# A one-core transformer block: weight steps paced by product, each unit's first product moved up one place, and a reload cut into pieces

## The chip, the core and the metric

The kernel runs on one core of a Trainium2 chip. A core has engines that run side by side, each with its own queue of instructions in a fixed order: TensorE (PE) multiplies matrices, VectorE (DVE) and ScalarE (ACT) work on whole tiles, GpSimd (POOL) is little used here, and SyncE (SP) issues all transfers between the core's memory and DRAM. An engine that comes to an instruction whose inputs are not there stands still, with all that is queued behind it. PE writes its sums into PSUM banks of 128 x 512 numbers, and ACT and DVE take them out.

The metric is the device time of one execution in microseconds (us). The kernel before takes 2230.76 us, the median of three runs (2227.21 to 2230.81).

## What is computed

The input is a matrix x of 1024 tokens x 1024 features, in 32-bit floats. The block normalises it, projects it with one wide matrix, mixes tokens in two ways, merges, and adds a squared-ReLU network:

```python
xn = rmsnorm(x, norm1_g[l])
qa, ka, va, qr, kr, vr, gr, gate_a, gate_b = [xn @ wl[:, bounds[i]:bounds[i + 1]] for i in ...]
# o_a: dilated sliding-window attention, 12 heads of 128, mixed over three groups
# o_r: retention, 4 heads, keys of 256, values of 512, in chunks of 128 tokens
y = jax.nn.sigmoid(gate_a) * (o_a @ w_proj_a[l]) + jax.nn.sigmoid(gate_b) * (o_r @ w_proj_b[l])
x = x + y @ w_out[l]
x = x + jnp.square(jax.nn.relu(rmsnorm(x, norm2_g[l]) @ w_up[l])) @ w_down[l]
```

## The kernel before, in words

**Numbers in two parts.** Every operand of a large product is split into a high part (`wh`, `xh`), which ACT writes as a rounded copy (line 330), and a low part (`wl`, `xl`), which DVE writes as the difference (line 333). A product of two such operands takes three matmuls: high x high, high x low and low x high.

**Units of seven products.** The projections from the normalised input, the second projection and the up projection are done in units of 256 output features with a fast scheme in the manner of Strassen: seven products N1 to N7 instead of eight. A product is 12 matmuls (4 blocks of the sum x 3). N1 and N2 of a unit are summed in one PSUM bank, N6, N7 and N4 in a second, N5 and N3 in a third (`BANK`). The bank of N6, N7 and N4 begins as minus N1: ACT copies N1's result there, negated (line 398), and only then may N2 go on summing on N1's bank. N6 and N7 are copied out by ACT too (lines 403 and 406).

**Order on PE.** PE's order is the program's. `strassen_order` gives it: two units' N1 and N2 first, then for each unit j the products N6, N5, the N1 of unit j+2, N7, the N2 of unit j+2, N4 and N3. There are 36 input units, 252 products: the q and k of the 12 attention heads (a unit for each head), eight units of the retention's gate `gr`, eight of the merging gates, and eight of the retention's q and k (`rqk`). The second projection (eight units, called "pb") has its own list in the same order. The other engines' orders are made by a scheduler from the program's order, except for instructions that are told to keep their place.

**Weights.** The class `Weights` holds a list of weight steps. A unit has two raw tiles of 512 KB each, loaded by SP (line 182) into a ring, and four steps: A is for N1 and N2, and D, B and C for the rest. C is for N5 and N7. A step splits one raw tile, or half of one, into its two parts; behind step D, DVE also forms the sums of the raw quarters (line 123) that B and C need. There are two buffers for A, two for B, and one for C. When a product was the last user of a buffer, `free` calls `pump`, which carries out all steps whose buffer is free, requesting raw tiles as the ring allows. So a split can be put in order directly behind the request of its own raw tile.

**Attention beside the units.** From product 138 on, the 12 heads' attention runs in small matmuls between those of the unit products. `plan_core` hangs actions on product numbers (`on(p, ...)`). For head n with p0 = 138 + 9 n, the q and k of its first 512 tokens (c = 0) are requested at p0 - 4 and those of the last (c = 1) at p0. `scale` multiplies q (f = 0) or k (f = 1) on DVE by its norm (line 705); it was due at p0 - 2 and p0 - 1 for c = 0, and at p0 + 2 and p0 + 3 for c = 1. Scores (line 642) need the scaled q and k. DVE adds a bias and takes the minimum (line 645), ACT takes the exponential (line 647), PE turns the result, ACT copies it out (line 657, `pT`), and PE multiplies by the values.

**Where the retention begins.** The retention needs the fourth quarter of the normalised input, `XS[0, 1]`, in its chunks 4 to 7 of each head. It was put aside in DRAM (`xs_d`) when its place was wanted, and is loaded back as two transfers of 1 MB (line 910). Each of the 32 chunks needs its q and k (`rqT`, `rkT`, 128 KB each, line 902) from DRAM; PE uses them at line 933. They are issued two chunks ahead.

Stages: start and values up to about 141 us, input units 141 to 971 (attention from 557), retention to 1310, first projection to 1340, second projection to 1490, output projection to 1605, up to 1890, down to the end.

Of the kernel before, what the change touches and what calls it, by code (L numbers as in the profile page):

```python
# [10 lines left out]
F = mybir.dt.float32  # L11
# [26 lines left out]
class Weights:  # L38
# [12 lines left out]
    def __init__(self, nc, rawp, wp, split):  # L51
        self.nc, self.rawp, self.wp, self.split = nc, rawp, wp, split
        self.raw, self.used, self.next = [], set(), 0
        self.src, self.steps = [], []
        self.place, self.more = [], None
        self.last = {}
        self.units, self.done = {}, set()
        self.plain = self.taken = 0
        self.cycle, self.turn = tuple(range(self.WB)), 0

        self.places = {}
        self.limit, self.keep, self.first = None, None, {}

    def claim(self, buf, key):

# [30 lines left out]
    def add_units(self, tag, srcs, flip=0):  # L96

        base = len(self.src)
        self.first[tag] = len(self.steps)
        kept = {}  # L100
        for s in srcs:
            self.place += [(len(self.src) + i - base) % (self.RAW + 1) for i in range(2)]
            self.src += [s[0], s[1]]

        def piece(key, buf, r, cols, then=None):
            def step():
                if isinstance(buf, tuple):
                    if not kept:
                        kept["D"] = self.buffer(buf[0])
                    h, l = (x[:, 512 * buf[1]:512 * buf[1] + 512] for x in kept["D"])  # L110
                else:
                    h, l = self.buffer(buf)
                self.split(h, l, self.raw[r][:, cols], key[0] == "up" and key[1] < 2 and key[2] != "A")
                self.units[key] = h, l
                if then:
                    then()

            self.steps.append((self.claim(buf, key), r, step))

        def sums(r):  # L120
            (x22, x21), (x11, x12) = ((self.raw[i][:, 0:512], self.raw[i][:, 512:1024]) for i in (r, r + 1))
            for x, y in ((x22, x21), (x21, x11), (x11, x22), (x12, x11)):
                ins = self.nc.vector.tensor_tensor(x, x, y, op=OP.add)
                if tag == "up" and r <= base + 2:
                    self.keep(ins)

        both = slice(0, 1024)
        for j in range(-1, len(srcs)):
            if j + 1 < len(srcs):
                r = base + 2 * (j + 1)  # L130
                piece((tag, j + 1, "A"), self.A[(j + 1) % 2], r + 1, both)
            if j >= 0:
                r = base + 2 * j
                piece((tag, j, "D"), (self.D, j % 2), r, slice(0, 512), lambda r=r: sums(r))
                piece((tag, j, "B"), self.B[(j + flip) % 2], r + 1, both, lambda r=r: self.used.add(r + 1))
                piece((tag, j, "C"), self.C, r, both, lambda r=r: self.used.add(r))
        m = len(srcs) + flip
        self.cycle = (0, 1, self.B[m % 2], self.C, self.D, self.B[(m - 1) % 2])
        self.turn = 0
# [32 lines left out]
    def load(self):  # L172
        n = len(self.raw)
        if n >= len(self.src):
            return False
        b = self.place[n]
        if any(self.place[m] == b and m not in self.used for m in range(max(0, n - 8), n)):
            return False
        if b == self.RAW and self.more is None:
            return False  # L180
        raw = (self.more if b == self.RAW else self.rawp).tile([P, UW], F, name=f"raw{b}", bufs=1)
        self.nc.sync.dma_start(raw[:, :self.src[n].shape[1]], self.src[n])
        self.raw.append(raw)
        return True

    def pump(self, most=99):
        while most > 0 and self.next < len(self.steps) and self.next != self.limit:
            before, r, step = self.steps[self.next]
            if before - self.done:
                return  # L190
            while len(self.raw) <= r:
                if not self.load():
                    return
            step()
            self.next += 1
            while self.load():
                pass
            most -= 1
# [4 lines left out]
        return list(range(lo, lo + count))  # L203

    def __getitem__(self, i):
        return self.units[i]

    def free(self, *ids):
        self.done.update(ids)
        self.pump()  # L210


class Pipe:


    def __init__(self, nc):
        self.nc = nc
        self.slot = 0
        self.due = {}

# [17 lines left out]
    def step(self, ps, terms, ends=None, first=True):  # L238
        fns = self.due.pop(self.slot, [])
        n, m = len(terms), len(fns)  # L240
        place = {}
        for j, fn in enumerate(fns):
            place.setdefault(min(n - 1, (j + 1) * n // (m + 1)), []).append(fn)

        def after(i):
            for fn in place.get(i, []):
                fn()
            if ends and i in ends:
                ends[i]()

        self.group(ps, terms, after, first)
        self.slot += 1

# [5 lines left out]
BANK = {"N1": "a", "N2": "a", "N6": "b", "N7": "b", "N4": "b", "N5": "d", "N3": "d"}  # L261


def strassen_order(units):


    order = [(0, "N1"), (1, "N1"), (0, "N2"), (1, "N2")]
    for j in range(units):
        late = j + 3 >= units
        order += [(j, "N6"), (j, "N5")] + ([] if late else [(j + 2, "N1")]) + [(j, "N7")]  # L270
        order += [(j + 2, "N2")] if not late else [(units - 1, ("N1", "N2")[j + 3 - units])] if j + 1 < units else []
        order += [(j, "N4"), (j, "N3")]
    return order
# [3 lines left out]
def hybrid_block(ctx: ExitStack, tc: tile.TileContext, a: dict, out: bass.AP):  # L277
    nc = tc.nc
# [89 lines left out]
    for nb in range(2):  # L368
        for u in range(4):
# [5 lines left out]
                 [{"N1": 0, "N2": 1, "N3": 2, "N5": "n2a", "N7": "n2b", "N6": 5, "N4": 4},  # L375
                  {"N1": "y1a", "N2": "n3a", "N3": "n3b", "N5": 3, "N7": "w1a", "N6": "w1b", "N4": "w1c"}])
    pipe = Pipe(nc)

    def product(tag, j, name, unit, operands, pu, result):

# [294 lines left out]
    def plan_core():  # L675
# [62 lines left out]
        for n in range(HEADS):  # L738
            p0 = FIRST + EACH * n
            on(p0 - 1, lambda n=n: prepare(n))  # L740
            for c in range(2):
                on(p0 - 4 + 4 * c, lambda n=n, c=c: bring(n, c))
                for f in range(2):
                    on(p0 - 2 + 4 * c + f, lambda n=n, c=c, f=f: scale(n, c, f))
            for b in range(NT):
                p, m = p0 + b, NT * n + b
                if b % 2 == 0:
                    on(p, lambda n=n, b=b: fetch(n, b))
                on(p, lambda n=n, b=b: begin(n, b))
                on(p, lambda m=m: pipe.at(3, lambda: turned(m)))  # L750
                on(p, lambda m=m: pipe.at(0, stages[m][0]))
# [16 lines left out]
    with ExitStack() as ph:  # L768
# [74 lines left out]

        unit = {}
        NIN = NA + NG + NQ + 8
        first = W.take(4)
        for p, (j, name) in enumerate(strassen_order(NIN)):
            if p == FIRST - 4:
                sqs.close()
                plan_core()  # L850
            for fn in events.pop(p, []):
                fn()
            product("in", j, name, unit, operands, lambda: pu, result)
            if (j, name) == (NIN - 1, "N7"):
                start = values(first, slice(0, P), False)
        assert not events
        W.more = None
    gst.close()


# [25 lines left out]
    with ExitStack() as ph:  # L886
# [19 lines left out]

        load_chunk(0)
        load_chunk(1)
        for i, x in enumerate(XS[0, 1]):
            tc.keep_in_program_order(nc.sync.dma_start(x.bitcast(F).rearrange("p a b -> p (a b)"), xs_d[i]))  # L910
        places = [x for i in range(2) for x in as_rows(XS[i, 0])]
        oaS = [(places[2 * p][:, i], places[2 * p + 1][:, i]) for p in range(2) for i in range(2)]

# [5 lines left out]
        for h in range(RH):  # L919
# [4 lines left out]
            for c in range(NT):  # L924
                ts = slice(c * P, (c + 1) * P)
                load_chunk(NT * h + c + 2)
                qT, kT, sr = ready.pop(NT * h + c)
                it = {}

# [112 lines left out]
    with ExitStack() as ph:  # L1042
        ES, e1, exts = None, ExitStack(), ExitStack()
        OPB = [{"N5": XS[0, 1], "N7": XS[1, 1]}, {}]
        waiting = [("N7", 1)] + [(name, h) for name in ("N1", "N2", "N6") for h in range(2)]
        sigmoid(gates[0])
        for n, (d, cs) in enumerate(work):
            if not cs.start:
# [39 lines left out]
        pm3 = pool(ph, "pm3", 10)  # L1088
        order = [(0, "N1"), (1, "N1"), (0, "N2"), (1, "N2")]
        for j in range(6):  # L1090
            order += [(j, "N6"), (j, "N5"), (j + 2, "N1"), (j, "N7"), (j + 2, "N2"), (j, "N4"), (j, "N3")]
        order += [(6, "N6"), (6, "N5"), (6, "N7"), (7, "N6"), (6, "N4"), (7, "N5"), (7, "N7"), (6, "N3"), (7, "N4"),
                  (7, "N3")]
        results = [(j, *{"N2": (0, 0), "N7": (1, 1), "N4": (1, 0), "N3": (0, 1)}[name])
# [60 lines left out]
        for i, (j, name) in enumerate(order):  # L1155
# [11 lines left out]
            if (j, name) in fetched:  # L1167
                u = fetched[j, name]
                late[u] = loaded(pm3, yl_d[u - 4], "s")
        assert not todo and not begun and not late  # L1170
        e1.close()


# [387 lines left out]
```

## Time and profile before

| | before |
|---|---|
| median of three runs | 2230.76 us |
| the profiled execution | 2229.98 us |
| its span, first to last instruction | 2228.2 us |
| granted TensorE clock, mean | 0.996 |
| busy: PE, DVE, ACT, POOL | 2174.8, 1390.9, 1127.4, 330.5 us |
| moved by DMA | 359.09 MB, 161 GB/s on average |

How to read the rows of the next sections. A row of a timeline gives start, length, engine, line of the kernel, operation, output and inputs with sizes, and in brackets the idle time before it and what ended it. SPq rows are transfers issued by SP. A row of waits gives the engine, its tile and line, what it waited for, the total in us, how often, and the longest. A row of stages gives the window, its length, for PE, PE's weight loads, DVE, ACT and POOL the busy time with the number of instructions, then the granted clock, the DMA share and GB/s. "mm" and "ms" are the PSUM banks of products, "tr" those of small matmuls and transposes.

### The profile page before, as it was taken

To read this page: it belongs to the slowest core of one execution; us is meant where nothing else is said; L and a number is where in the kernel's file an instruction comes from. 1 tells how busy PE (TensorE), PEld (TensorE's weight loads), DVE (VectorE), ACT (ScalarE), POOL (GpSimd) and SP (SyncE) were. 2 spreads that over 40 slices of the span, in tenths; PEclk is the share of its full clock that TensorE was granted. 3 is DMA by queue.
4 is the path that set the end of the run, shared out by engine and by line. 5 is a ranking of instruction groups with operands and counts; after the bars stand their busy time and mean duration, and the time that the engine had idled before them with its cause. 6 is when DMAs were issued, how large, how long until landed. Compare 5 with 4: busy or idle time off the path is not lost. (4 is left out here: it accounts for less than half of the span.)

```text
span 2228.2 us, 28853 instructions
## 1 busy us (share of the span) xinstructions
PE 2174.8 (98%) x9928; PEld 1785.4 (80%) x9928; DVE 1390.9 (62%) x2374; ACT 1127.4 (51%) x2145; POOL 330.5 (15%) x340
## 2 busy tenths in 40 slices
PE   8999999999999999999999999999899999999999
PEld 6888888787888888878888877778788888778777
DVE  5624554655555665648776867793855556787874
ACT  4425665544654544535555645552555545755542
POOL 0000000000000000002133120000000000677873
PEclk9999999999999999999999999999999999999999
DMA  6323333333657667664364478774255556644533
GB/s 205 133 85 91 99 102 97 96 133 111 199 169 219 207 197 216 186 193 129 113 199 119 133 254 267 258 239 153 86 147 154 153 149 201 225 166 160 179 122 104
DMA packets 293750, 359.09 MB, mean 161 GB/s; under 512 B 34962, under 2 KB 202322, under 8 KB 293091
## 3 DMA queue, kind: packets, MB, share of 16 engines
q1 hardware_dynamic: 293602, 357.25, 51.2%
q8 instruction: 78, 1.28, 0.2%
q14 instruction: 70, 0.57, 0.1%
HBM read 240.59 MB, written 116.59 MB: 160 GB/s over the span
## 5 line engine op out<-in xcount | busy, mean ns | idle before, releaser
L333 DVE TENSOR_TENSOR wl<-raw,wh 128x1024 fp32r<-128x1024 f32 (+1 forms) x308 | 345.4, 1123 | 384.9 <-ACT wh L330 384.2
L330 ACT ACTIVATE wh<-raw 128x1024 fp32r<-128x1024 f32 (+1 forms) x308 | 295.8, 962 | 278.7 <-PE ms L229 98.1
L229 PE MATMUL mm<-xh,wh 128*128 128x512 f32 x960 | 390.4, 407 | 10.2 <-ACT ms L398 9.7
L229 PE MATMUL mm<-xh,wl 128*128 128x512 f32 x960 | 376.3, 392 | 0.0
L229 PE MATMUL mm<-xl,wh 128*128 128x512 f32 x960 | 376.0, 392 | 0.3 <-DVE xl L333 0.3
L229 PE MATMUL ms<-xh,wh 128*128 128x512 f32 x784 | 317.5, 405 | 5.1 <-DVE s L1059 1.6
L229 PE MATMUL ms<-xh,wl 128*128 128x512 f32 x784 | 306.7, 391 | 0.0
L229 PE MATMUL ms<-xl,wh 128*128 128x512 f32 x784 | 306.2, 391 | 0.0
L229 PEld LDWEIGHTS mm<-xh,wh 128*128 128x128 f32 x960 | 181.5, 189 | 49.1 <-ACT ms L398 13.8
L229 PEld LDWEIGHTS mm<-xh,wl 128*128 128x128 f32 x960 | 181.0, 189 | 39.2
L229 PEld LDWEIGHTS mm<-xl,wh 128*128 128x128 f32 x960 | 181.7, 189 | 34.6 <-DVE xl L333 0.7
L966 POOL TENSOR_TENSOR st<-st,half 128x1 f32<-128x1 f32 x32 | 26.7, 833 | 1102.8 <-DVE st L965 1102.7
L229 PE MATMUL mm<-wh,xh 128*128 128x512 f32 x458 | 187.5, 409 | 1.8 <-ACT xh L330 1.4
L229 PE MATMUL mm<-wh,xl 128*128 128x512 f32 x458 | 180.9, 395 | 0.3 <-DVE xl L333 0.3
L229 PE MATMUL mm<-wl,xh 128*128 128x512 f32 x458 | 179.8, 393 | 0.0
L229 PEld LDWEIGHTS ms<-xh,wh 128*128 128x128 f32 x784 | 147.5, 188 | 37.4 <-ACT u L406 5.0
L229 PEld LDWEIGHTS ms<-xh,wl 128*128 128x128 f32 x784 | 147.4, 188 | 31.9
L229 PEld LDWEIGHTS ms<-xl,wh 128*128 128x128 f32 x784 | 147.7, 188 | 27.3
L229 PEld LDWEIGHTS mm<-wh,xl 128*128 128x128 f32 x458 | 86.6, 189 | 20.2 <-DVE xl L333 0.8
L229 PEld LDWEIGHTS mm<-wh,xh 128*128 128x128 f32 x458 | 87.0, 190 | 18.7 <-ACT xh L330 1.8
L229 PEld LDWEIGHTS mm<-wl,xh 128*128 128x128 f32 x458 | 87.2, 190 | 15.9
L1392 DVE TENSOR_TENSOR Y<-Y,ms 128x512 f32<-128x512 f32 x88 | 59.7, 682 | 55.6 <-PE ms L229 55.5
(304 smaller groups left out, 3984.8 us busy)
## 6 DMA issues: line engine op xcount, KB each, us to landing
raw<-in_w_up SPq DMA_DIRECT2D x32, 512.0 KB
h_d<-s SPq DMA_DIRECT2D x64, 256.0 KB
raw<-in_w_down SPq DMA_DIRECT2D x32, 512.0 KB
raw<-in_w_aqk_q SPq DMA_DIRECT2D x24, 512.0 KB
qk_d<-sg SPq DMA_DIRECT2D x48, 256.0 KB
qk<-qk_d SPq DMA_DIRECT2D x24, 512.0 KB
rb<-rs_d SPq DMA_DIRECT2D x24, 512.0 KB
s<-sg_d SPq DMA_DIRECT2D x40, 256.0 KB
```

Of the source, the lines that this page charges most:

```text
L229: self.nc.tensor.matmul(ps, x, y, start=start, stop=stop, skip_group_check=not first)
L330: hi = nc.scalar.activation(dst_h, src, AF.Copy)
L333: nc.vector.tensor_tensor(dst_l, src, dst_h.bitcast(F), op=OP.subtract)
L966: nc.gpsimd.tensor_tensor(st[:, 9:10], st[:, 8:9], half[:, 0:1], op=OP.pow)
L1392: nc.vector.tensor_tensor(Y[r][:, ns], Y[r][:, ns], ps, op=op)
```

## The change

**Pace.** `Weights` gets a clock that `Pipe.step` moves on with each product. In the input units and the second projection a weight step may be placed only two products after its raw tile was requested (`lag` 2), and at most one step per product (`pace` 1); `free` then places none itself. In the retention the lag is 1 and there is no pace; before the output projection both are switched off, and what is ready is placed at once. A weight that is asked for before its step was placed brings the step on at once, without lag.

**Raw pairs.** The two raw tiles of a unit are requested in the other order, the one with A first.

**N1 one place up.** In the input units and the second projection, the N1 of unit j+2 comes before unit j's N5 instead of after. The up projection keeps its order.

**Scales.** `scale` of c = 0 is due at p0 - 1 for q and k both; c = 1 keeps p0 + 2 and p0 + 3.

**Reload in pieces.** The two transfers of 1 MB become eight of 256 KB, written in the program at chunks 1 to 3 of the retention's first head, three at a time; the scheduler may set them earlier.

```diff
@@ class Weights, add_units
-            self.src += [s[0], s[1]]
+            self.src += [s[1], s[0]]
...
@@ class Weights, load
         self.raw.append(raw)
+        self.born.append(self.clock)
         return True
...
@@ class Weights, pump
             while len(self.raw) <= r:
                 if not self.load():
                     return
+            if self.clock < self.born[r] + self.lag:
+                return
             step()
...
     def __getitem__(self, i):
+        while i not in self.units:
+            lag, self.lag, at = self.lag, 0, self.next
+            self.pump(1)
+            self.lag = lag
+            assert self.next > at
         return self.units[i]

     def free(self, *ids):
         self.done.update(ids)
-        self.pump()
+        if self.pace is None:
+            self.pump()
+
+    def tick(self):
+        self.clock += 1
+        if self.pace is not None:
+            self.pump(self.pace)
...
@@ class Pipe, step
         self.slot += 1
+        self.tick()
...
-def strassen_order(units):
+def strassen_order(units, soon=False):
...
-        order += [(j, "N6"), (j, "N5")] + ([] if late else [(j + 2, "N1")]) + [(j, "N7")]
+        ahead = [] if late else [(j + 2, "N1")]
+        order += [(j, "N6"), *(ahead if soon else []), (j, "N5"), *([] if soon else ahead), (j, "N7")]
...
-                    on(p0 - 2 + 4 * c + f, lambda n=n, c=c, f=f: scale(n, c, f))
+                    on(p0 - 1 + 3 * c + f * c, lambda n=n, c=c, f=f: scale(n, c, f))
...
+        W.lag, W.pace = 2, 1
         first = W.take(4)
-        for p, (j, name) in enumerate(strassen_order(NIN)):
+        for p, (j, name) in enumerate(strassen_order(NIN, True)):
...
         W.more = None
+        W.lag, W.pace = 1, None
...
-        for i, x in enumerate(XS[0, 1]):
-            tc.keep_in_program_order(nc.sync.dma_start(x.bitcast(F).rearrange("p a b -> p (a b)"), xs_d[i]))
+        back = [(k, i) for k in range(4) for i in range(2)]
...
                 load_chunk(NT * h + c + 2)
+                for _ in range(3 if back and c else 0):
+                    k, i = back.pop(0) if back else (None, None)
+                    if i is not None:
+                        nc.sync.dma_start(XS[0, 1][i][:, k].bitcast(F), xs_d[i][:, 512 * k:512 * k + 512])
...
+        W.lag, W.pace = 2, 1
         sigmoid(gates[0])
...
-            order += [(j, "N6"), (j, "N5"), (j + 2, "N1"), (j, "N7"), (j + 2, "N2"), (j, "N4"), (j, "N3")]
+            order += [(j, "N6"), (j + 2, "N1"), (j, "N5"), (j, "N7"), (j + 2, "N2"), (j, "N4"), (j, "N3")]
...
+        W.lag, W.pace = 0, None
+        W.pump()
         e1.close()
```

What this does to the engines' orders is shown at three places. Line numbers of the changed file are up to some 40 higher: 347 for 330, 350 for 333, 416 for 398, 421 for 403, 424 for 406, 723 for 705, 922 for 902.

The first place is ACT's queue around the copy of unit 13's N1 (`ms<-mm`); `u2` and `u3` are the copies of unit 11's N6 and N7, `wh0` the high part of the next A, `wh5` that of C. Before:

```order
L403 ACTIVATE u2_3082<-ms_2799 128x512
L330 ACTIVATE wh0_3148<-raw1_3146 128x1024
L398 ACTIVATE ms_3112<-mm_3097 128x512
L330 ACTIVATE wh5_3140<-raw0_2831 128x1024
L406 ACTIVATE u3_3128<-ms_2799 128x512
```

After:

```order
L421 ACTIVATE u2_3084<-ms_2786 128x512
L416 ACTIVATE ms_3099<-mm_3086 128x512
L347 ACTIVATE wh0_3176<-raw0_3082 128x1024
L347 ACTIVATE wh5_3154<-raw1_2845 128x1024
L424 ACTIVATE u3_3130<-ms_2786 128x512
```

The copy, which stood behind the A split, stands ahead of it.

The second is DVE's queue just before the first attention head: `qk` are its q and k, `rb` their norms, `sg` a gate, `wl3` the low part of a B, and the raw tiles are being summed. Before:

```order
L123 TENSOR_TENSOR raw1_3984<-raw1_3984,raw0_3982 128x512
L123 TENSOR_TENSOR raw1_3984<-raw1_3984 128x512
L705 SCALAR_TENSOR_TENSOR qk_4133<-qk_4133,gqk_107,rb_4134 128x512
L835 TENSOR_TENSOR sg_4188<-u2_4063,sg_4188 128x512
L333 TENSOR_TENSOR wl3_4193<-raw1_3984,wh3_4192 128x1024
L705 SCALAR_TENSOR_TENSOR qk_4133<-qk_4133,gqk_107,rb_4134 128x512
```

After:

```order
L124 TENSOR_TENSOR raw0_3927<-raw0_3927,raw1_3996 128x512
L124 TENSOR_TENSOR raw0_3927<-raw0_3927 128x512
L853 TENSOR_TENSOR sg_4187<-u2_4065,sg_4187 128x512
L723 SCALAR_TENSOR_TENSOR qk_4123<-qk_4123,gqk_107,rb_4124 128x512 x2
L350 TENSOR_TENSOR wl3_4208<-raw0_3927,wh3_4207 128x1024
```

Both scales now stand together, ahead of the low part (x2 is two in a row).

The third is SP's queue where the retention begins: `rqT_8182`, `rkT_8183` and `sr_8186` are chunk 0's loads before (`rqT_8176`, `rkT_8177`, `sr_8180` after), `rqT_8188` and `rkT_8189` chunk 1's, `raw` of `in_w_rv` a value weight, `rqk_d<-u2_8035` the store of the last q and k. Before, with `xl<-xs_d` as the next row:

```order
L902 DMA rqT_8182<-rqk_d_83 128x2x128
L902 DMA rkT_8183<-rqk_d_83 128x2x128
L904 DMA sr_8186<-sr_d_84 128x4x128
L842 DMA rqk_d_83<-sg_8124 128x512
L182 DMA raw1_8131<-in_w_rv 128x1024
L491 DMA oa_d_81<-oaT_8145 128x256
L842 DMA rqk_d_83<-u2_8035 128x512
L182 DMA raw2_8157<-in_w_rv 128x1024
L902 DMA rqT_8188<-rqk_d_83 128x2x128
L902 DMA rkT_8189<-rqk_d_83 128x2x128
L904 DMA sr_8192<-sr_d_84 128x4x128
L910 DMA xh_8171<-xs_d_92 128x2048
```

After, with one more piece (`xh`) ahead of these rows, and `rkT_8183` as the next row behind them:

```order
L949 DMA xl_8166<-xs_d_92 128x512
L949 DMA xh_8165<-xs_d_92 128x512
L949 DMA xl_8166<-xs_d_92 128x512
L949 DMA xh_8165<-xs_d_92 128x512
L922 DMA rqT_8176<-rqk_d_83 128x2x128
L922 DMA rkT_8177<-rqk_d_83 128x2x128
L924 DMA sr_8180<-sr_d_84 128x4x128
L860 DMA rqk_d_83<-sg_8124 128x512
L182 DMA raw1_8149<-in_w_rv 128x1024
L509 DMA oa_d_81<-oaT_8139 128x256
L860 DMA rqk_d_83<-u2_8035 128x512
L922 DMA rqT_8182<-rqk_d_83 128x2x128
```

Five pieces stand ahead of chunk 0's loads, the second value weight is gone from between the store and chunk 1's loads (it comes behind chunk 4's), and the last three pieces stand behind chunk 4's loads as well.

More of the change, by code (lines that the diff above doesn't have):

```diff
@@ L62, in __init__ @@
         self.limit, self.keep, self.first = None, None, {}
+        self.clock, self.lag, self.pace, self.born = 0, 0, None, []
     def claim(self, buf, key):
@@ L120, in sums @@
         def sums(r):
-            (x22, x21), (x11, x12) = ((self.raw[i][:, 0:512], self.raw[i][:, 512:1024]) for i in (r, r + 1))
+            (x22, x21), (x11, x12) = ((self.raw[i][:, 0:512], self.raw[i][:, 512:1024]) for i in (r, r - 1))
             for x, y in ((x22, x21), (x21, x11), (x11, x22), (x12, x11)):
                 ins = self.nc.vector.tensor_tensor(x, x, y, op=OP.add)
-                if tag == "up" and r <= base + 2:
+                if tag == "up" and r <= base + 3:
                     self.keep(ins)
@@ L129, in add_units @@
             if j + 1 < len(srcs):
-                r = base + 2 * (j + 1)
-                piece((tag, j + 1, "A"), self.A[(j + 1) % 2], r + 1, both)
+                piece((tag, j + 1, "A"), self.A[(j + 1) % 2], base + 2 * (j + 1), both)
             if j >= 0:
-                r = base + 2 * j
+                r = base + 2 * j + 1
                 piece((tag, j, "D"), (self.D, j % 2), r, slice(0, 512), lambda r=r: sums(r))
-                piece((tag, j, "B"), self.B[(j + flip) % 2], r + 1, both, lambda r=r: self.used.add(r + 1))
+                piece((tag, j, "B"), self.B[(j + flip) % 2], r - 1, both, lambda r=r: self.used.add(r - 1))
                 piece((tag, j, "C"), self.C, r, both, lambda r=r: self.used.add(r))
@@ L217, in __init__ @@
         self.nc = nc
+        self.tick = None
         self.slot = 0
@@ L377, in hybrid_block @@
     pipe = Pipe(nc)
+    pipe.tick = W.tick
     def product(tag, j, name, unit, operands, pu, result):
```

## The prediction

> **What bounds the kernel now.** I read the page's first lines, then a table by stage, then what PE waits for, and then the timeline at each wait that the edits touch.
>
> ```profile
> core 0: 2228.2 us, clock 0.996
> ...
> PE 2174.8 (98%) x9928; PEld 1785.4 (80%) x9928; DVE 1390.9 (62%) x2374; ACT 1127.4 (51%) x2145; POOL 330.5 (15%) x340
> ...
> 150.00:550.00 400.00, 396.91 (x1741) 326.36 (x1740) 215.23 (x280) 218.29 (x317) 0.00 (x0) 1.00 0.34 106
> 550.00:970.00 420.00, 411.19 (x2060) 343.26 (x2059) 243.02 (x651) 212.13 (x569) 0.00 (x0) 1.00 0.65 194
> 970.00:1310.00 340.00, 331.72 (x1594) 273.47 (x1593) 247.86 (x546) 182.65 (x378) 80.02 (x96) 0.99 0.53 156
> ...
> 1340.00:1490.00 150.00, 144.51 (x628) 117.35 (x629) 118.56 (x169) 81.85 (x129) 0.00 (x0) 1.00 0.80 265
> ...
> 1605.00:1890.00 285.00, 284.27 (x1246) 235.36 (x1247) 169.16 (x219) 150.10 (x235) 4.98 (x4) 0.99 0.53 156
> ```
>
> PE bounds it: 98% busy at full clock. No matmul is removed, so only PE's idle time and its slow stretches can go: 3.1 us in the input units before attention (150 to 550), 8.8 with attention (550 to 970), 8.3 in the retention, 5.5 in the second projection (1340 to 1490), together 25.7 us, and what the clock costs behind the longest waits. That is the ceiling of a gain, a little over 1%.
>
> ```profile
> PE mm L229 <- ACT ms L398: 9.7, 8, 2.5
> ...
> PE tr L642 <- DVE qk L705: 3.5, 4, 1.9
> ...
> PE ms L933 <- DMA rkT<-rqk_d: 3.5, 1, 3.5
> ...
> ACT wh L330 <- DMA raw<-in_w_up: 55.7, 13, 4.6
> ```
>
> The first three are PE's own waits that the edits reach. The last is a warning: ACT stands 55.7 us for weights in the up stage, where PE is busy 284.27 of 285 us, so a blocked ACT costs nothing by itself. What costs is the instruction queued behind it, if PE wants it soon.
>
> **The change part by part.** *The first product one place up, and the weight steps behind it.* A unit's N2 accumulates on N1's bank, which ACT must first copy out (L398). At 405.91 this was late:
>
> ```profile
> 399.03 0.58 ACT L403 ACTIVATE u<-ms 128x512 f32<-128x512 f32 x1
> ...
> 399.89 0.35 SPq L182 DMA_DIRECT2D raw<-in_w_gr_q  x1
> ...
> 404.31 1.06 ACT L330 ACTIVATE wh<-raw 128x1024 fp32r<-128x1024 f32 x1 [4.71 <-DMA raw<-in_w_gr_q]
> 405.28 0.58 ACT L398 ACTIVATE ms<-mm 128x512 f32<-128x512 f32 x1
> ...
> 405.91 0.51 PE L229 MATMUL mm<-xh,wh 128*128 128x512 f32 x1 [0.83 <-ACT ms L398]
> ```
>
> The load was requested at 399.89, ACT stood at its split until 404.31, and the copy behind it came at 405.28. In the changed order the copy stands ahead of that split (shown with the change), and between N1 and N2 lie two products, 24 matmuls of about 0.23 us (396.91 us for 1741 in the first stage), instead of one. Either would cover 0.83 us. What is moved is 12 matmuls and one copy of 0.58 us; no DMA goes with it, and SP and POOL are not passed. The moved product needs its A weights 2.7 us sooner, which are split about a unit (seven products) ahead; at the second projection's start they are not. All eight such waits:
>
> ```profile
> 505.83 0.50 PE L229 MATMUL mm<-xh,wh 128*128 128x512 f32 x1 [1.26 <-ACT ms L398]
> ...
> 715.64 0.50 PE L229 MATMUL mm<-xh,wh 128*128 128x512 f32 x1 [0.86 <-ACT ms L398]
> ...
> 842.74 0.50 PE L229 MATMUL mm<-xh,wh 128*128 128x512 f32 x1 [1.35 <-ACT ms L398]
> ...
> 1342.16 0.50 PE L229 MATMUL mm<-xh,wh 128*128 128x512 f32 x1 [2.46 <-ACT ms L398]
> ...
> 1346.64 0.51 PE L229 MATMUL mm<-xh,wh 128*128 128x512 f32 x1 [1.46 <-ACT ms L398]
> ...
> 1399.99 0.50 PE L229 MATMUL mm<-xh,wh 128*128 128x512 f32 x1 [0.87 <-ACT ms L398]
> ...
> 1439.28 0.50 PE L229 MATMUL mm<-xh,wh 128*128 128x512 f32 x1 [0.64 <-ACT ms L398]
> ```
>
> The one at 1342.16 belongs to the projection's unit 0, whose copy still stands behind the first B split: it stays, 2.46. At 1346.64 unit 1's copy goes ahead of its B split, but unit 2's N1 then meets its own A split; I take 0.8 of 1.46. At 1439.28 the copy stood behind splits of activations, and the extra product helps only if those come no later: half, 0.32. The others go whole: 0.83 + 1.26 + 0.86 + 1.35 + 0.8 + 0.87 + 0.32 = 6.3 us. The bounds are 0 and the whole 9.7 less 2.46, which is 7.3.
>
> *The scales one event later, and a load asked for earlier.* The scales of q and k (L705) stand on DVE among the weights' low parts (0.75 beside 1.23 us each):
>
> ```profile
> 555.91 1.23 DVE L333 TENSOR_TENSOR wl<-raw,wh 128x1024 fp32r<-128x1024 f32 x1
> 557.05 0.75 DVE L705 SCALAR_TENSOR_TENSOR qk<-qk,gqk,rb 128x512 f32<-128x512 f32 x1
> ...
> 557.86 0.49 PE L642 MATMUL tr<-qk 128*128 128x128 f32 x2 [0.73 <-DVE qk L705]
> ...
> 571.72 0.46 PE L642 MATMUL tr<-qk 128*128 128x128 f32 x2 [0.90 <-issue]
> ...
> 927.82 0.49 PE L642 MATMUL tr<-qk 128*128 128x128 f32 x2 [1.86 <-DVE qk L705]
> ...
> 919.95 1.06 ACT L330 ACTIVATE wh<-raw 128x1024 fp32r<-128x1024 f32 x1 [3.03 <-DMA raw<-in_w_rv]
> ...
> 928.00:932.00 4.00, 4.00 (x13) 3.19 (x14) 3.14 (x17) 1.60 (x5) 0.00 (x0) 0.57 0.40 109
> ```
>
> At 557.86 both scales now stand ahead of the low part of 1.23 us: 0.73 goes. At 571.72 the A split comes ahead by a product, and I count half, 0.45. The wait of 1.86 at 927.82 came of a chain: ACT stood 3.03 us for a value weight, its low part and the raw sums came late on DVE, and the scale behind them. The changed order asks for that weight some two products sooner and puts the scale ahead of those sums, so it goes, and with it the slow clock behind it: 4 us at 0.57 are 1.72 us lost. Sum 0.73 + 0.45 + 1.86 + 1.72 = 4.8 us, bounds 0 and 5.2. The other scales that move stand a product later on DVE, whose 38% of free time covers their 0.75 us: nothing; without that cover each would cost what the wait at 557.86 did.
>
> [...]
>
> *The reload in pieces.* Where the retention begins, PE waits for chunk 1's k:
>
> ```profile
> 961.67 0.33 SPq L842 DMA_DIRECT2D rqk_d<-u  x1
> ...
> 967.14 0.37 SPq L902 DMA_DIRECT2D rqT<-rqk_d  x1
> 967.57 0.46 SPq L902 DMA_DIRECT2D rkT<-rqk_d  x1
> ...
> 970.83 0.32 SPq L842 DMA_DIRECT2D rqk_d<-u  x1
> 972.22 0.33 SPq L182 DMA_DIRECT2D raw<-in_w_rv  x1
> ...
> 973.11 0.64 SPq L902 DMA_DIRECT2D rkT<-rqk_d  x1
> ...
> 974.30 0.50 SPq L910 DMA_DIRECT2D xh<-xs_d  x1
> ...
> 971.97 0.61 PE L933 MATMUL ms<-rqT,rkT 128*128 128x128 f32 x4
> ...
> 978.38 0.69 PE L933 MATMUL ms<-rqT,rkT 128*128 128x128 f32 x4 [3.48 <-DMA rkT<-rqk_d]
> ...
> 978.00:982.00 4.00, 3.62 (x14) 3.02 (x15) 1.40 (x4) 1.30 (x4) 0.00 (x0) 0.68 1.04 420
> ```
>
> It was issued at 973.11, behind a weight of 512 KB and with the two megabyte loads right behind it, and landed 5.3 us later. Now five pieces of 256 KB stand ahead of chunk 0's loads, where SP was idle from 961.67 to 967.14; the weight goes behind, and chunk 1's k directly follows the store of 970.83, so at about 971.8. Chunk 0's k, issued at 967.57, was there when used at 971.97, 4.4 us at most. Between 3.5 and 4.4 us of flight it lands at 975.3 to 976.2, against 974.90 wanted (978.38 less 3.48): 0.8 us stay, bounds 0 and 3.48. A wait so short has no slow stretch behind it at 505.83 (1.26 us), so the 1.3 us (4 x 0.32) of the last row and some 0.4 us after it go too. Gain 3.48 + 1.7 - 0.8 = 4.4 us, bounds 0 and 5.2. The six added issues take about 0.5 us of SP each, in its idle time. The last three pieces stand behind chunk 4's loads, which are made two chunks ahead; chunks 4 to 7 use them, and two chunks are some 21 us (340 us for 32), so their landing is covered.
>
> *What it costs.* Steps come at ticks, at most one a product. In "in" each split was ready well ahead of its use, so a product's delay is covered. But with attention the A split now stands on ACT one product earlier, and behind it an exponential (L647) and the copies L406 and L657. No row shows this order. Its price where uncovered is that of the wait at 715.64, 0.86; three such places among the 16 units that run beside attention (420 us hold products 136 to 251, 3.6 us each, seven to a unit) give 2.6 us; the ends are 0 and 16 x 0.86 = 13.8 us. I take three because a product there lasts 3.6 us against a flight of 4.4, and the requests stand mostly over a product ahead. The swap of the two halves of a raw pair, and the final pump before the up stage, move no wait: nothing.
>
> Sum: 6.3 + 4.8 + 4.4 - 2.6 = 12.9 us. The profiled execution took 2229.98; 2217.1 for it, and as it stands 0.78 below the median shown, 2217.9.
>
> **The rivals.** *Waits change places* (2229.1): the A split ahead of the exponentials stalls PE once in each of the 16 units, 13.8 in place of 2.6 us, leaving 15.5 - 13.8 = 1.7. For it: the wait at 405.91 is of that kind, with ACT 4.71 us at a split. Against: in the order the split mostly stands more than a product behind its request.
>
> *The reload stays* (2222.3): the pieces in flight hold up chunk 0's loads, or chunk 1's k again takes 5.3 us; the 4.4 us are lost and the rest holds. For it: the DMA share in the last row is 1.04. Against: 1.25 MB at the 420 GB/s of that row take 3.0 us, over by 967.
>
> *Slower* (2236): the delayed D, B or C splits reach PE too late. One late split costs 1.06 + 1.23 = 2.3 us; eight units of the 44 give 18.4 us, net 5.5 slower; it decides from six late units, where 12.9 are used up. Against: C is free at N7 and next used at N5, now five products later instead of four.
>
> **How the numbers follow.** A measurement of this kernel tells about 0.2%, 4.5 us. Chances: my forecast 0.52 (own range 2212 to 2224), the reload stays 0.18, waits change places 0.17, slower 0.13. The first two are faster, 0.70; the third is the same. The range starts at 2211, all gains in full (7.3 + 5.2 + 5.2) and a little of other waits, and ends at 2232 beyond the third case.
>
> **What would show it.** Right: in PE's waits ms L398 falls to some 3 us, with 1342 left; no wait for rkT over 1.5 us and no granted clock under 0.9 around 928 and 980; ACT's waits for raw of the gr and rqk weights no longer precede the copy. Wrong: new waits of PE for u L406 or for acc and pT after 560, longer ones for xl or wl, or PE idle at 967 to 972.

## The result, and the profile after

The changed kernel takes 2217.52 us (median of six runs, 2214.82 to 2220.47) against 2229.12 for the kernel before (2225.89 to 2230.81): a ratio of 0.995 with a 95% interval of 0.9937 to 0.9963, so 11.6 us faster. The forecast was 2217.9.

The profiled execution of the changed kernel, 2214.82 us, is the fastest of its six. Its first lines and its stages (window, length, then PE, weight loads, DVE, ACT and POOL, clock, DMA share, GB/s):

```profile
core 0: 2213.0 us, clock 0.998
...
PE 2168.8 (98%) x9928; PEld 1783.6 (81%) x9928; DVE 1387.4 (63%) x2374; ACT 1128.4 (51%) x2145; POOL 329.8 (15%) x340
...
150.00:550.00 400.00, 398.65 (x1751) 327.95 (x1750) 217.64 (x284) 219.01 (x318) 0.00 (x0) 1.00 0.35 107
550.00:970.00 420.00, 412.26 (x2078) 345.37 (x2076) 243.01 (x654) 213.52 (x570) 0.00 (x0) 1.00 0.67 202
```

The span fell by 15.2 us, in two parts. PE's idle time went from 53.4 us (2228.2 less 2174.8) to 44.2 (2213.0 less 2168.8), 9.2 less. Its busy time went down by 6.0 with the same 9928 instructions. Read in windows of 2 us, the granted clock falls to 0.50 in four stretches before (1.7 us lost behind 928, 1.7 behind 978, 3.4 behind 1604, 1.7 behind 1948) and in two after (1.7 behind 814, 3.4 behind 1588), which is 3.4 us less; what made the other 2.6 us of busy time is open.

The stretch behind 1948 lies in the down stage, which no edit touches: PE waits 2.05 us there before and 2.39 after, with a slow stretch only before. So 1.7 us of this trace's gain are luck. In the six runs the time goes with the mean clock, from 2214.82 us at 0.998 to 2220.47 at 0.996.

What PE waited for, in the changed kernel (L416 there is L398 before, L424 is L406, L663 is L645):

```profile
PE ms L244 <- ACT u L424: 3.7, 6, 1.0
PE mm L244 <- DVE wl L350: 2.7, 3, 1.6
...
PE tr L506 <- DVE acc L663: 2.5, 1, 2.5
PE ms L956 <- DMA rkT<-rqk_d: 2.2, 1, 2.2
PE tr L660 <- DVE acc L663: 2.0, 2, 1.3
```

No row for the copy of N1 is left (9.7 us before), and none for the scales (3.5 before). The wait for chunk 1's k went from 3.5 to 2.2. But there are new ones: 4.5 us behind DVE's L663, 2.7 for a weight's low part (1.6 of it at 1486, where the kernel before waited 1.4 for the high part of an input at 1501), and 3.7 instead of 1.6 for the copy of N7.

The copy of unit 13's N1 and the split behind it, on ACT:

```profile
399.04 0.58 ACT L421 ACTIVATE u<-ms 128x512 f32<-128x512 f32 x1
399.51 0.59 ACT L416 ACTIVATE ms<-mm 128x512 f32<-128x512 f32 x1
404.49 1.06 ACT L347 ACTIVATE wh<-raw 128x1024 fp32r<-128x1024 f32 x1 [4.38 <-DMA raw<-in_w_gr_q]
```

ACT still stands 4.38 us for the weight, but the copy is done at 400.1, 5.8 us sooner than before, and PE does not wait for it. The first attention head's scales, on DVE:

```profile
552.54 1.41 DVE L723 SCALAR_TENSOR_TENSOR qk<-qk,gqk,rb 128x512 f32<-128x512 f32 x2
553.86 1.22 DVE L350 TENSOR_TENSOR wl<-raw,wh 128x1024 fp32r<-128x1024 f32 x1
...
554.27 0.38 PE L660 MATMUL tr<-qk 128*128 128x128 f32 x2
```

Both are done before the low part, and the scores start without idle time. The start of the retention:

```profile
963.08 0.32 SPq L860 DMA_DIRECT2D rqk_d<-u  x1
963.45 0.49 SPq L922 DMA_DIRECT2D rqT<-rqk_d  x1
963.99 0.76 SPq L922 DMA_DIRECT2D rkT<-rqk_d  x1
...
969.32 0.68 PE L956 MATMUL ms<-rqT,rkT 128*128 128x128 f32 x4 [2.19 <-DMA rkT<-rqk_d]
```

Chunk 1's k was in use 5.33 us after its issue (its flight), as long as before (978.38 less 973.11 is 5.27). What became shorter is the way from the store to the issue: 0.9 us (963.99 less 963.08) instead of 2.3.

The costliest new wait, where DVE stands at a scale:

```profile
805.66 0.55 SPq L715 DMA_DIRECT2D rb<-rs_d  x1
...
808.33 1.23 DVE L350 TENSOR_TENSOR wl<-raw,wh 128x1024 fp32r<-128x1024 f32 x1 [0.26 <-ACT wh L347]
813.24 0.75 DVE L723 SCALAR_TENSOR_TENSOR qk<-qk,gqk,rb 128x512 f32<-128x512 f32 x1 [3.68 <-DMA rb<-rs_d]
813.90 0.42 DVE L663 CUSTOM_DVE_ANT_0 s<-tr,bias 128x256 f32<-128x256 f32 x1
...
814.38 0.69 PE L506 MATMUL tr<-ident,oa 128*128 128x128 f32 x2 [2.55 <-DVE acc L663]
...
814.00:818.00 4.00, 3.62 (x11) 2.95 (x12) 2.46 (x7) 2.48 (x7) 0.00 (x0) 0.57 0.87 298
```

DVE stood 3.68 us for norms issued at 805.66. Behind the scale in its queue stood the row of L663 that PE waited for. A slow stretch followed, of the size of the one at 928 before (0.57 over 4 us in both). At the same place of the kernel before, the two rows stood the other way round:

```profile
817.66 1.23 DVE L333 TENSOR_TENSOR wl<-raw,wh 128x1024 fp32r<-128x1024 f32 x1 [0.26 <-ACT wh L330]
818.80 0.42 DVE L645 CUSTOM_DVE_ANT_0 s<-tr,bias 128x256 f32<-128x256 f32 x1
...
821.68 0.75 DVE L705 SCALAR_TENSOR_TENSOR qk<-qk,gqk,rb 128x512 f32<-128x512 f32 x1 [2.45 <-DMA rb<-rs_d]
```

There too DVE stood at the scale for norms, 2.45 us, but the scores were done, and PE did not wait. Over the whole kernel DVE stood even longer for norms before (32.2 us against 21.1). So the new wait comes of the order on DVE, not of a longer stand. Of the 4.5 us behind L663, 3.2 lie behind a scale (at 814 and 870); the other 1.3 at 847 lie behind L663's own bias, for which DVE stood 4.96 us.

### The profile page after: what moved, and what is told of

Read it like the earlier page. It is cut to its first block, busy times and chain, and to the rows that moved or that the text cites. A ratio compares the mean times of both kernels' runs of the same rounds, so it can differ in the third digit from the quotient of the medians.

```text
span 2213.0 us, 28838 instructions
## 1 busy us (share of the span) xinstructions
PE 2168.8 (98%) x9928; PEld 1783.6 (81%) x9928; DVE 1387.4 (63%) x2374; ACT 1128.4 (51%) x2145; POOL 329.8 (15%) x340
```

## The experiments

Each run is given by its ratio to the kernel before, with the 95% interval. There were three groups of four kernels, each with runs of the kernel before beside it (2229.27, 2227.29 and 2227.08 us), so times are compared within a group, and ratios across groups.

### Each part alone

N1 alone, on the kernel before:

```diff
-        order += [(j, "N6"), (j, "N5")] + ([] if late else [(j + 2, "N1")]) + [(j, "N7")]
+        ahead = [] if late else [(j + 2, "N1")]
+        order += [(j, "N6"), *(ahead if soon else []), (j, "N5"), *([] if soon else ahead), (j, "N7")]
...
-        for p, (j, name) in enumerate(strassen_order(NIN)):
+        for p, (j, name) in enumerate(strassen_order(NIN, True)):
...
-            order += [(j, "N6"), (j, "N5"), (j + 2, "N1"), (j, "N7"), (j + 2, "N2"), (j, "N4"), (j, "N3")]
+            order += [(j, "N6"), (j + 2, "N1"), (j, "N5"), (j, "N7"), (j + 2, "N2"), (j, "N4"), (j, "N3")]
```

> The kernel before with only N1 moved one place up (input units and second projection). Here ACT's copy of N1 still stands behind the A split, but two products lie between N1 and N2. Theory (the added product is the cover): PE's waits for ms L398 fall from 9.7 to about 3 us and the time by about 6 us, to some 2223. Rival (the copy must also stand ahead of the split, which takes the lag): the waits stay above 6 us, and the time falls by under 2 us.

Measured: 2221.36 us against 2229.27, ratio 0.9964 (0.9951 to 0.9976), 7.9 us faster.

```profile
PE ms L934 <- DMA rkT<-rqk_d: 3.9, 1, 3.9
...
PE mm L229 <- ACT ms L399: 3.7, 2, 2.2
PE tr L643 <- DVE qk L706: 3.5, 4, 1.9
```

Waits for the copy fell from 9.7 to 3.7 us; the two left are those at the start of the second projection (2.2 and 1.5). My premise, that the copy still stands behind the split, was wrong at the place I had looked at:

```profile
400.28 0.59 ACT L399 ACTIVATE ms<-mm 128x512 f32<-128x512 f32 x1
404.54 2.19 ACT L331 ACTIVATE wh<-raw 128x1024 fp32r<-128x1024 f32 x2 [3.67 <-DMA raw<-in_w_gr_q]
```

Moving N1 is enough to bring its copy ahead of the split; the lag is not needed for it. This is so almost everywhere: of the 44 copies of N1 up to the end of the second projection, 19 stood before in an unbroken row behind a split that had waited for its weight, with N1 alone 2, and with lag, pace and pairs alone (the next run) still 19. So the run does not tell the cover of a second product from the copy's new place.

Lag, pace and swapped pairs alone (the changed classes `Weights` and `Pipe` and the lines that set `W.lag, W.pace`; order, scales and reload as before):

> The kernel before with only lag, pace and the swapped raw pairs. N1 is where it was, and its copy still stands behind the A split. Theory: the waits for ms L398 stay near 9.7 us; the wait of 1.9 us near 928 with the slow clock behind it goes, so the time falls by 3 to 4 us, to some 2226. Rival: steps that come later give the gain back, no change within 1 us.

Measured: 2221.85 us, ratio 0.9963 (0.995 to 0.9976), 7.4 us faster, twice what I expected.

```profile
PE mm L244 <- ACT ms L416: 6.5, 8, 1.3
...
PE tr L506 <- DVE acc L663: 3.1, 2, 2.2
...
PE tr L660 <- DVE acc L663: 2.1, 3, 0.8
PE ms L953 <- DMA rkT<-rqk_d: 2.0, 1, 2.0
```

The wait behind the scale near 928 is gone, as expected. So are the two long waits for the copy at the start of the second projection (the longest left is 1.3 us), which I had not expected. And the wait for chunk 1's k is 2.0, with the reload as it was. The new waits behind L663 are here too, 5.2 us of them, so they come with this group of edits. At the place shown above the scale stands ahead of the scores in this trace as well (818.54 and 819.21). So with the weight steps placed later the scheduler sets the two the other way round; why it does was not looked at.

Scales alone:

```diff
-                    on(p0 - 2 + 4 * c + f, lambda n=n, c=c, f=f: scale(n, c, f))
+                    on(p0 - 1 + 3 * c + f * c, lambda n=n, c=c, f=f: scale(n, c, f))
```

> The kernel before with only the scales of c = 0 due one product later. Theory: the wait of 0.7 us at 558 goes, nothing else: 0.7 us faster at most. Rival: the scales come too late for the scores, or the queue behind them changes, and PE's waits for qk L705 grow from 3.5 us: 1 to 3 us slower.

Measured: 2228.45 us, ratio 0.9993 (0.9984 to 1.0001): 0.8 us, not told from nothing.

```profile
PE tr L642 <- DVE qk L705: 3.4, 3, 1.9
...
555.93 0.49 PE L642 MATMUL tr<-qk 128*128 128x128 f32 x2 [1.33 <-DVE qk L705]
925.96 0.49 PE L642 MATMUL tr<-qk 128*128 128x128 f32 x2 [1.87 <-DVE qk L705]
```

The wait at the first head is still there, even longer, and so is the one near 928. With lag, pace and pairs alone both were gone but for 0.2 us.

Reload in pieces alone (the reload's lines of the change, on the kernel before):

> The kernel before with only the reload in eight pieces. Theory: the wait for rkT falls from 3.5 us to 2 us or less and the slow clock behind it goes: 3 to 4 us faster. Rival: the flight of chunk 1's k is 5.3 us whatever lies around it, and it is issued no earlier, because a value weight still stands ahead of it: the wait stays at 3.5 us and the time within 1 us.

Measured: 2229.25 us, ratio 1.0002 (0.9992 to 1.0011): nothing.

```profile
970.19 0.32 SPq L842 DMA_DIRECT2D rqk_d<-u  x1
971.58 0.33 SPq L182 DMA_DIRECT2D raw<-in_w_rv  x1
971.97 0.45 SPq L902 DMA_DIRECT2D rqT<-rqk_d  x1
972.47 0.47 SPq L902 DMA_DIRECT2D rkT<-rqk_d  x1
...
978.04 1.23 PE L936 MATMUL ms<-rqT,rkT 128*128 128x128 f32 x4 [3.79 <-DMA rkT<-rqk_d]
```

The megabyte loads no longer stand behind chunk 1's k, and its flight is still over 5 us (972.47 to 978.04). The value weight still stands ahead of it, issued 1.4 us behind the store, so chunk 1's k is issued as late as before, 2.3 us behind the store, and PE waits 3.79 us. The rival was right.

The four gains add up to 16.1 us, where the whole change gives 11.6 (13.7 in the last group below).

### What in the pace, and what of the reload

The changed kernel with the reload as two transfers again:

```diff
-        back = [(k, i) for k in range(4) for i in range(2)]
+        for i, x in enumerate(XS[0, 1]):
+            tc.keep_in_program_order(nc.sync.dma_start(x.bitcast(F).rearrange("p a b -> p (a b)"), xs_d[i]))
...
-                for _ in range(3 if back and c else 0):
...
```

> The changed kernel with the reload as two transfers of 1 MB again. Theory (what shortened the wait for chunk 1's k is that the pace took the value weight from ahead of it, not the pieces): PE waits some 2 us for rkT, no slow clock behind it, and the time stays within 1 us of the changed kernel's 2217.5. Rival (the pieces are needed once the order is right): the wait goes back to 3.5 us or more with a slow clock behind it, 2221 or more.

Measured: 2213.26 us against 2227.29, ratio 0.9934 (0.9922 to 0.9946). It is not slower than the changed kernel (0.995, 0.9937 to 0.9963), so the rival is out. By the ratios it is 3.6 us faster, more than the 1 us of the theory, but the intervals overlap. The theory holds for the wait, which is 1.93 us, and not for the clock: a slow stretch does follow.

```profile
967.15 1.07 PE L953 MATMUL ms<-rqT,rkT 128*128 128x128 f32 x4 [1.93 <-DMA rkT<-rqk_d]
...
968.00:972.00 4.00, 4.00 (x15) 3.29 (x14) 1.27 (x4) 1.27 (x3) 0.00 (x0) 0.66 1.00 396
```

The swapped raw pairs alone:

```diff
-            self.src += [s[0], s[1]]
+            self.src += [s[1], s[0]]
... (the places in the steps that count the raw tiles follow)
```

> The kernel before with only the two raw tiles of a unit requested in the other order. Theory (pace and lag carry the 7.4 us of the run with pace alone): within 1.5 us of the kernel before, the wait of 1.9 us near 928 stays. Rival (the swap is what brings the A split's data sooner): 4 us or more faster, waits for ms L398 down to 7 us or less.

Measured: 2226.93 us, ratio 0.9995 (0.9984 to 1.0005): no change in time, as expected. But waits did move. Those for the copy were 7.6 us instead of 9.7. The wait near 928, which I had expected to stay, fell from 1.86 to 0.78 us (at 926.59). Against that stand 2.0 us behind DVE's scores (the row that is L663 in the changed kernel), which the kernel before does not show, and 4.2 us instead of 1.6 for the copy of N7. So part of the new waits may come of the swap. The wait for chunk 1's k was 3.7.

Pace without lag (as lag and pace alone, with every lag 0):

> The kernel before with pace and the swapped pairs, but a lag of 0. Theory (one step per product is what moves the value weights and spreads the steps; the lag of two only keeps a split away from its own request): as fast as with the lag within 1.5 us, some 2222. Rival (the lag is what matters): splits stand behind their own request again, waits for ms L398 at 9 us or more, and the time above 2226.

Measured: 2224.36 us, ratio 0.9983 (0.9972 to 0.9993), 2.9 us faster. With the lag the ratio was 0.9963 (0.995 to 0.9976). The intervals touch, and the two ran in different groups, so that the lag is worth about as much as the pace is likely and not shown. Neither theory nor rival holds whole: PE waits 7.0 us for the copy, less than before, and 1.7 for chunk 1's k, so the pace takes the value weight away without the lag. But two waits that are gone with the lag are back: 2.06 us for the copy at the start of the second projection, and 1.6 us for the state (St) at the retention's end.

The attention's requests one product sooner, in the changed kernel:

```diff
-                on(p0 - 4 + 4 * c, lambda n=n, c=c: bring(n, c))
+                on(max(p0 - 5 + 4 * c, FIRST - 4), lambda n=n, c=c: bring(n, c))
```

> The changed kernel with the q, k and norms of each attention half requested one product sooner (from p0 - 5 and p0 - 1). The changed kernel has new waits of PE for DVE's L663 (2.5, 1.3 and 0.7 us), where DVE stood 3.7 and 3.3 us at a scale whose norms were in flight. Theory: those behind a scale (2.5 and 0.7) go or halve, and the time falls by 2 to 3 us, to some 2215. Rival: the earlier request waits for the buffer's last reader on SP and holds up what is behind it; no change, or slower.

Measured: 2214.74 us, ratio 0.9941 (0.9926 to 0.9955), by the ratios 2 us less than the changed kernel, with overlapping intervals. The waits moved:

```profile
DVE qk L723 <- DMA rb<-rs_d: 14.2, 7, 3.0
...
PE tr L660 <- DVE acc L663: 2.9, 3, 1.6
...
PE tr L660 <- DVE qk L723: 1.3, 1, 1.3
```

DVE stands 14.2 us for norms instead of 21.1, and PE 2.9 us behind L663 instead of 4.5, but 1.3 us at a scale are new. Another 0.3 us behind L663 makes it 4.5 us again: the waits were moved, not shortened. So the rival was right that PE gains nothing here; whether for the reason it gave (SP held up) was not looked at.

### Together, on one chip

Four kernels ran beside each other, to tell what the parts are worth together: the changed kernel; the one with the reload as two transfers; N1, lag, pace and pairs without scales and pieces; and the changed kernel with two transfers and the earlier requests.

> The changed kernel as it is, beside the next three on one chip. Theory: 11 to 13 us faster than the kernel before.

> The changed kernel with the reload as two transfers of 1 MB, on the same chip as the changed kernel. Theory (the pieces are worth nothing): within 1.5 us of the changed kernel. Rival (the pieces cost): 2 us or more faster than it, as the first runs on two different chips gave.

> The kernel before with N1 moved and pace, lag and swapped pairs; scales and reload as before. Alone these two gave 7.9 and 7.4 us. Theory (each removes waits of its own, and pace brings some 5 us of new waits at the attention's DVE queue only once): 11 to 13 us faster than before, as fast as the changed kernel within 1.5 us. Rival (the sum holds, and scales or pieces cost some 4 us together): 15 us faster.

> The changed kernel with the reload as two transfers and the attention's q, k and norms requested one product sooner. Theory: the earlier request takes 1 to 2 us off the waits behind DVE's scales, the reload nothing: 2 us faster than the changed kernel. Rival: as the changed kernel within 1 us.

Measured, against 2227.08 us for the kernel before:

| kernel | us | ratio | 95% interval |
|---|---|---|---|
| changed | 2213.34 | 0.994 | 0.9928 to 0.9953 |
| two transfers | 2216.07 | 0.9947 | 0.9934 to 0.9961 |
| N1, lag, pace, pairs | 2215.96 | 0.9953 | 0.9941 to 0.9966 |
| two transfers, earlier requests | 2215.09 | 0.994 | 0.9926 to 0.9954 |

All four intervals overlap. N1 with lag, pace and pairs makes 11.1 us of the changed kernel's 13.7 here; for both 11 to 13 was expected. The 2.6 us left for scales and pieces are not told from nothing. Two transfers were 2.7 us slower than the changed kernel, where the groups before had them 3.6 faster: neither theory nor rival came. The earlier requests, expected to be 2 us faster, were 1.8 slower. No version was found that is clearly faster than the changed kernel. The two parts alone gave 7.9 and 7.4, together 11.1. Where the difference of some 4 us goes was not settled; it is not much above what runs differ by. The new waits behind L663 are in all four (4.7 us without scales and pieces, 3.3 in this group's run of the changed kernel).

## Why the prediction was right, and where it was not

**The total** was right, 2217.9 for 2217.5, and partly by luck, because errors cancel. In the profiled execution I had forecast 9.4 us less idle time of PE and 3.4 us less slow clock; measured were 9.2 and 3.4, made up otherwise. The waits that I named gave 15.4 us instead of 12.0, and the costs were 9.3 instead of 2.6. Some 3 us net came of waits that no term names, among them 1.6 for St at the retention's end and 1.5 at the kernel's start, where other traces show from nothing to 1.6.

**N1.** The term was 6.3 us, the run with this part alone gave 7.9 (5.4 to 10.9 by its interval). The size was right, and that the move of N1 takes these waits away. Whether by the second product or by the copy's place ahead of the split is open. Of the eight waits, six went by this part (of the one at 1439 I had counted half); I was right that 1342 stays with it, and wrong that 0.8 us would go at 1346. The one at 1346 went with the pace, the one at 1342 only where the lag was there too, so in the changed kernel all 9.7 us are gone.

**Scales and the earlier request.** The waits told of are all gone in the changed kernel (3.5 us at the scales, and the slow stretch at 928, 1.7), so 4.8 was near. But I put the first of them on the scales' new due time. Alone that gave 0.8 us, not told from nothing, with the wait at the first head still standing at 1.33 us. It goes with lag, pace and pairs. Of the wait near 928 the swapped pairs alone took 1.1 us. I had said of that swap that it moves no wait: it gave no time, but it moved several.

**The reload.** This is the step that failed. "Now five pieces of 256 KB stand ahead of chunk 0's loads" gave nothing (ratio 1.0002). The wait fell by 1.3 us, not by 2.7, and for another reason: "the weight goes behind", which the pace does. I had put two edits' effects in one term, since both were in the same rows of SP's order. And the flight of 3.5 to 4.4 us, taken from chunk 0's k, was wrong: chunk 1's k took 5.3 us before and after, 5.6 (978.04 less 972.47) where the megabyte loads were out of its way, and 5.1 with lag, pace and pairs alone (issue at 972.20, use at 977.31), where they stood right behind it. So they do not set that time. What does stays open; it was not tried with the store away.

**What it costs.** I took 2.6 us for A splits ahead of exponentials. The changed trace shows little of that; it shows 4.5 us behind DVE's L663, most of it where a scale whose norms are in flight has come to stand ahead, besides 2.1 us more at the copy of N7 and 2.7 at low parts. So 2.6 us stood where 9.3 were, and 7.2 of these were waits for DVE, not for ACT. The excess of the first term (9.7 for 6.3) made up for half of that, the waits that no term names for most of the rest.

**The clock.** The slow stretches at 928 and behind k's wait went in the changed kernel's trace, as told, a new one came at 814, and the one at 1948 was missing by luck. Behind k's wait the slow stretch is there in six of the eight other traces in which that wait is 1.7 to 2.3 us long (0.66 over 4 us behind 1.96 us with pace alone, 0.66 behind 1.93 with two transfers), so that term too was partly luck (last section). The rivals: waits did change places, but took 9.3 us where that case needs 13.8; "the reload stays" was right about the pieces and wrong about the time; the late splits of the slower case did not come in the sizes feared, 2.7 us against 18.4. Of the signs of being wrong, three came: waits for L424 (L406 before), for L663's acc and for low parts; and k's wait was 2.2 us, over the 1.5 named.

## What to carry to other kernels

When several edits touch the same queue, ask for each row which edit moved it: here the transfer that was in the way was moved by the weights' pace, and the edit that named the reload did nothing. When work is moved within a queue, look for what else changes places there: here a scale whose norms were still on their way came to stand ahead of scores that PE wanted, and 3.2 us of the gain were given back. An instruction that another engine wants soon should be put in order ahead of one that waits for a transfer, even if its engine then waits as long: where the scores stood ahead, DVE stood 2.45 us at the scale behind them and PE did not wait; where the scale stood ahead, DVE stood 3.68 us and PE 2.55.

## What was not expected of the hardware

A wait of PE of about 2 us is sometimes followed by a slow stretch and sometimes not, at the same place of the program. Near 925 the wait was 1.86 us before and 1.85 with N1 alone; the 4 us behind it ran at 0.57 before, and with N1 alone at full clock:

```profile
922.62 0.49 PE L643 MATMUL tr<-qk 128*128 128x128 f32 x2 [1.85 <-DVE qk L706]
...
923.00:927.00 4.00, 4.00 (x21) 3.39 (x21) 3.34 (x18) 1.85 (x6) 0.00 (x0) 1.00 0.38 101
```

For chunk 1's k, a wait of 1.96 us with pace alone was followed by 0.66 in the next 4 us, and one of 2.19 in the changed kernel by 1.00. The rows of both:

```profile
977.31 0.68 PE L953 MATMUL ms<-rqT,rkT 128*128 128x128 f32 x4 [1.96 <-DMA rkT<-rqk_d]
...
977.00:981.00 4.00, 3.69 (x14) 3.09 (x15) 1.40 (x4) 1.26 (x4) 0.00 (x0) 0.66 1.02 410
```

```profile
968.00:972.00 4.00, 2.68 (x15) 2.35 (x16) 1.74 (x5) 1.74 (x5) 0.00 (x0) 1.00 1.02 291
```

What decides whether a stretch follows a wait of that length is not shown by any run.

Over the 14 traces, from 140 us on, 21 of the 44 waits of 1.8 to 2.6 us had a slow stretch behind them, 3 of the 78 between 1.2 and 1.8, and all 19 of 3.4 us and more. Behind the shorter waits one stretch costs about 1.7 us, some 3.4 us at half the clock: 0.50 from 928.27 to 931.68 before, from 814.04 to 817.45 after (a window of 4 us shows less of it where it reaches beyond). So a single profiled execution can misjudge an edit by that much.
